# Four seven-product pairs instead of three in every second gate/up block, and plain pairs cut into halves, in a one-core float32 decoder layer

## The chip, the cores and the metric

The kernel runs on one core of a Trainium2 chip. Its time is device microseconds (us) from one launch; three runs gave 1085.74, 1085.87 and 1086.69 us, median 1085.87. Everything is computed to float32 accuracy: TensorE multiplies operands that were split into a high and a low part, and three matmuls make one product.

## The reference

A decoder layer for 256 tokens with width 2048: a combined input projection, a gated linear recurrence beside a retention head group, an output projection, and a SwiGLU feed-forward part of width 5632. The change concerns only the gate and up projections of the last part:

```
u = rmsnorm(h, ln2_w[l])
ff = jax.nn.silu(jnp.einsum('bsd,df->bsf', u, w_ffn_gate[l])) * jnp.einsum('bsd,df->bsf', u, w_ffn_up[l])
h = h + jnp.einsum('bsf,fd->bsd', ff, w_ffn_down[l])
```

with `u` 256x2048 and the gate and up weights 2048x5632 each, in float32.

## The kernel before

**Blocks, pairs and quads.** After the input part, the kernel is a list of blocks: two for the output projection (index 0 and 1), eleven for gate/up (index 2 to 12), two for the down projection. A gate/up block makes 512 gate and 512 up columns for all 256 tokens, in four PSUM banks c11, c12, c21 and c22 (token half by gate or up). It runs over the 2048 input rows in eight *pairs* of 128 rows each way; the weights of a pair are a *quad* of four 128x512 pieces, b11, b12, b22 and b21, loaded as two halves of 128x1024 (512 KB each).

**Products.** A *plain* pair takes eight products of a left piece (activations, 128x128) and a quad piece. A *summed* pair (table `SUMMED`) takes seven products, by sums of pieces on both sides. The sums of the left (s1 to s4) are made once and serve all blocks; the sums of the weights (t1 to t4) are made for each pair, by four VectorE additions in place (L648). A product is three matmuls in `three` (L670 high by high, L671 high by the low weights, L672 low by the high weights), so a plain pair has 24 matmuls and a summed one 21.

**Shared and direct steps.** The seven products of a summed pair stand in two places. Four of them are the *shared* step (`share`, 12 matmuls): they run one block ahead, while the block before is still accumulating in the other four banks, since they must be combined (L782 to L787) before plain products may be added to them. The other three are the *direct* step (`direct`, 9 matmuls), in the block itself; its pieces b22 and b21 are loaded a second time, and t4 is kept from the shared step. The string `STEPS` of a block gives the order: p a plain pair, s a shared step for the next block, d a direct step of this block.

**Making the weights ready.** Each piece is split by `split`: ScalarE casts the high part (L112), VectorE subtracts it from the raw weights for the low part (L113). Per pair this is:

- plain: two loads, two splits of 128x1024;
- shared: two loads, the split of b11 (128x512), the four additions, the splits of t1 with t3 (128x1024), of t2 and of t4 (128x512 each);
- direct: one load, one split of 128x1024.

The split pieces lie in pools of four buffers of 128x1024 for high (`wh`) and four for low parts (`wl`). A shared step holds two of each (b11 with t2, and t1 with t3), a direct step one, a plain pair two. t4 has buffers of its own. The raw weights have six buffers. A buffer is filled anew when the last instruction that reads it is done.

**What sets the order.** The program is written as a list of steps, with loads three halves ahead (`AHEAD`, L1086). A scheduler at build time then orders the instructions of each engine by its own estimate of times and gives out buffers as they come free; on the chip each engine runs its list in order and waits by semaphores. So three matmuls of one product may stand apart, and steps overlap by some matmuls.

Of the kernel before, what the change touches and what calls it, by code (L numbers as in the profile page):

```python
# [28 lines left out]

SUMMED = ((), (4, 5), (2, 3)) + ((1, 2, 3), (0, 1, 2, 3)) * 4 + ((1, 2, 3), (1, 2, 3))
SUMMED_OUT, SUMMED_FFN = (4, 5), (0, 1, 2, 3)

PLAIN = ((4, 5, 6, 7, 0, 1, 2, 3),) * 2 + (tuple(range(8)),) * 11
STEPS = ("pppspppspp", "ppspdpsdpp", "pdpsdpspspp") + ("pspsdpsdpsdp", "psdpsdpsddp") * 4 + ("psdpsdpsdpp", "psdpsdpsdpp")


EARLY_DOWN = (0, 1, 2)
# [5 lines left out]
def tile_hymba_layer(ctx: ExitStack, tc: tile.TileContext, A: dict, out: bass.AP):  # L45
# [17 lines left out]
    def nm(s):  # L63
        counter[0] += 1
        return f"{s}_{counter[0]}"
# [45 lines left out]
    def split(dst_h, dst_l, src):  # L111
        act.copy(out=dst_h, in_=src)  # L112
        v.tensor_tensor(out=dst_l, in0=src, in1=dst_h.bitcast(F32), op=ALU.subtract)  # L113

    class Unit:


        n_loads = 2

        def __init__(self, src, pieces=1, before=None, after=None):  # L120
            self.src, self.pieces, self.before, self.after = src, pieces, before, after
            self.h, self.l = [], []

        def load(self, j):
            raw = rpool.tile([P, 1024], F32, tag="raw", name=nm("raw"))
            h = wpool.tile([P, 1024], F32R, tag="wh", name=nm("wh"))
            l = wpool.tile([P, 1024], F32R, tag="wl", name=nm("wl"))
            n = 1024 // self.pieces
            for p in range(self.pieces):
                o = p * n  # L130
                nc.sync.dma_start(out=raw[:, o : o + n], in_=self.src[:, j * 1024 + o : j * 1024 + o + n])
                if self.before:
                    self.before(j * self.pieces + p)
            for p in range(self.pieces):
                o = p * n
                split(h[:, o : o + n], l[:, o : o + n], raw[:, o : o + n])
                if self.after:
                    self.after(j * self.pieces + p)
            self.h.append(h)
            self.l.append(l)  # L140
# [306 lines left out]
    half = {}  # L447
# [156 lines left out]
    class Quad:  # L604
# [3 lines left out]
        n_loads = 2  # L608
# [42 lines left out]
    EIGHT = (  # L651
        ("c11", "a11", "b11"), ("c12", "a11", "b12"), ("c22", "a21", "b12"), ("c21", "a21", "b11"),
        ("c11", "a12", "b21"), ("c12", "a12", "b22"), ("c22", "a22", "b22"), ("c21", "a22", "b21"),
    )
    LAST = tuple(e for c in ("c11", "c21", "c12", "c22") for e in EIGHT if e[0] == c)
# [7 lines left out]
    def room(m):  # L663

        return (aux, bank)[m % 2]
# [81 lines left out]
    class Direct(Quad):  # L747


        n_loads = 1  # L750
# [5 lines left out]
        def load(self, half):  # L756
# [2 lines left out]
            self.cut(("b22", "b21"), r)  # L759
            self.parts["t4"] = self.shared.parts["t4"]  # L760

    class Block:


# [25 lines left out]
            for c, a, b in DIRECT:  # L790
                three(self.ps[c], self.lefts[self.summed[m]][a], quad.parts[b], False, False, True)

        def plain(self, i, quad, first, last):
            ps, onto, seen = self.ps, bool(self.summed), set()
            for n, (c, a, b) in enumerate(LAST if last else EIGHT):
                if first and n == 4:
                    while turns:
                        turns.pop(0)()
                start = c not in ps
                if start:  # L800
                    ps[c] = room(self.index)(c)
                stop = last and c in seen
                three(ps[c], self.lefts[i][a], quad.parts[b], start, stop, onto)
                seen.add(c)
                if stop:
                    self.post(c, ps[c])

        def put(self, after):
            plain = [i for i in PLAIN[self.index] if i not in self.summed]
            for k, kind in enumerate(self.steps):  # L810
                if kind == "p":
                    i, n = plain.pop(0), len(plain)
                    quad = Quad(self.src(i), False)
                    run = lambda i=i, quad=quad, k=k, n=n: self.plain(i, quad, k == 0, n == 0)
                elif kind == "d":
                    m = self.steps[:k].count("d")
                    quad = Direct(self.shared[m])
                    run = lambda m=m, quad=quad: self.direct(m, quad)
                else:
                    m = self.steps[:k].count("s")  # L820
                    quad = after.shared[m]
                    run = lambda m=m: after.share(m)
                program.append(([quad], run))
# [209 lines left out]
    first = [True]  # L1033
# [31 lines left out]
    def swap():  # L1065
# [3 lines left out]

    blocks = [Block(d, lambda i, d=d: A["w_out"][8 * d + i], y, out_post(d), STEPS[d], SUMMED[d]) for d in range(2)]  # L1070
    blocks += [
        Block(2 + j, lambda i, j=j: A["w_gu"][8 * j + i], hh, ffn_post(j), STEPS[2 + j], SUMMED[2 + j])
        for j in range(NB)
# [15 lines left out]
    for step, (units, run) in enumerate(program):  # L1089
        need += sum(un.n_loads for un in units)  # L1090
        while done < min(len(loads), need + AHEAD):
            un, j = loads[done]
# [109 lines left out]
```

## Time and profile before

| | |
|---|---|
| median of three runs | 1085.87 us |
| span of the profiled execution (first to last instruction) | 1084.4 us |
| TensorE (PE) busy | 1074.2 us, 99%, 5101 matmuls |
| VectorE (DVE) busy | 953.5 us, 88%, 1371 instructions |
| ScalarE (ACT) busy | 660.9 us, 61%, 935 instructions |
| DMA read from HBM | 235.26 MB, 219 GB/s over the span |
| granted TensorE clock, mean | 0.999 |

The span is 1.5 us less than the median time; what lies before the first and behind the last instruction is not in it. Busy time of PE is time in which at least one matmul was running, and matmuls overlap: one takes about 0.39 us from start to end, but the next starts 0.23 us after it. The same holds in a small way for DVE: a 128x512 instruction lasts 0.69 us by the profile, and the next may start 0.60 us after it. Views by time stretch and the list of single instructions (start, duration, engine, line, operation, tiles) are used below; there the tile names stand without buffer numbers, so `wl<-raw,wh` is any split into a low part.

In the order of instructions, shown below and in the prediction's sense, names carry numbers: `c22_1343` is a bank, `wh_1330` and `wl_1331` are high and low split weights, `ah`/`al` the left operand's parts, `sh`/`sl` those of its sums, `t4h`/`t4l` the parts of t4, `raw_1357` loaded weights.

### The profile page before, as it was taken

What the parts mean: (1) busy time and instruction counts of PE and PEld (TensorE: products, weight loads), DVE (VectorE), ACT (ScalarE), POOL (GpSimd) and SP (SyncE); (2) the same over time, 40 slices, a digit from 0 to 9 for tenths busy, and PEclk for the clock granted to TensorE, in tenths of its full rate; (3) what the DMA queues carried; (4) which work ended last, traced back from release to release, by engine and by line L of the source; (5) the groups of instructions that cost most, each with busy time, mean ns of one, the idle gap of its engine ahead of it and who ended that gap; (6) DMA issues with size and microseconds to landing.
All of it is one profiled execution on the core that took longest, in us unless ns stands there. A gap on an engine that the chain in (4) does not pass through costs nothing.

```text
span 1084.4 us, 14584 instructions
## 1 busy us (share of the span) xinstructions
PE 1074.2 (99%) x5101; PEld 899.5 (83%) x5101; DVE 953.5 (88%) x1371; ACT 660.9 (61%) x935; POOL 51.0 (5%) x61
## 2 busy tenths in 40 slices
PE   9999999999999999999999999999999999999997
PEld 7888888888888788888888888888888888888885
DVE  7789799988878889888998998999899899898986
ACT  7666644468746676565566566556556666655563
POOL 0612230000000000000000000000000000000001
PEclk9999999999999999999999999999999999999999
DMA  9964474444565567577677677686675756465652
GB/s 330 333 211 168 160 252 173 174 175 171 181 230 205 184 228 275 198 248 266 220 245 261 220 264 235 233 289 214 233 271 194 265 181 213 171 214 199 212 209 85
DMA packets 69274, 238.32 MB, mean 220 GB/s; under 512 B 7888, under 2 KB 8272, under 8 KB 69200
## 3 DMA queue, kind: packets, MB, share of 16 engines
q1 hardware_dynamic: 68400, 235.29, 62.7%
q0 software_dynamic: 512, 1.57, 0.4%
q8 instruction: 40, 0.66, 0.2%
q10 hardware_dynamic: 288, 0.52, 0.1%
q14 instruction: 34, 0.28, 0.1%
HBM read 235.26 MB, written 2.10 MB: 219 GB/s over the span
## 4 chain that ended last, share of the span: by engine, by line
PE 97%; DVE 1%; issue 1%; DMA 0%; ACT 0%; POOL 0%; SPq 0%; POOLq 0%; ACTq 0%
PE c L670 22%; PE c L672 22%; PE c L671 22%; PE fm L184 11%; PE fm L186 5%; PE tm L164 3%; PE tm L165 3%; PE tm L166 3%; PE p L672 1%; PE p L671 1%; PE p L670 1%; PE ft L833 1%; DMA raw<-in_w_v 0%; PE ht L576 0%; PE sc L482 0%
## 5 line engine op out<-in xcount | busy, mean ns | idle before, releaser
L112 ACT CAST wh<-raw 128x1024 fp32r<-128x1024 f32 (+1 forms) x490 | 460.9, 965 | 362.6 <-PE c L672 132.5
L113 DVE TENSOR_TENSOR wl<-raw,wh 128x1024 fp32r<-128x1024 f32 (+1 forms) x490 | 538.2, 1122 | 91.2 <-ACT wh L112 88.4
L671 PE MATMUL c<-wl,ah 128*128 128x512 f32 x850 | 331.0, 390 | 0.0
L672 PE MATMUL c<-wh,al 128*128 128x512 f32 x850 | 330.4, 389 | 0.0
L670 PE MATMUL c<-wh,ah 128*128 128x512 f32 x850 | 275.0, 391 | 0.2 <-ACT wh L112 0.2
L670 PEld LDWEIGHTS c<-wh,ah 128*128 128x128 f32 x850 | 159.4, 188 | 33.4 <-ACT wh L112 1.1
L672 PEld LDWEIGHTS c<-wh,al 128*128 128x128 f32 x850 | 159.6, 188 | 33.0
L671 PEld LDWEIGHTS c<-wl,ah 128*128 128x128 f32 x850 | 159.6, 188 | 32.7
L184 PE MATMUL fm<-u,wh 128*128 128x512 f32 x512 | 161.3, 396 | 0.0
L186 PEld LDWEIGHTS fm<-u,wl 128*128 128x128 f32 x512 | 96.0, 188 | 22.5
L186 PE MATMUL fm<-u,wl 128*128 128x256 f32 x512 | 101.1, 278 | 0.0
L184 PEld LDWEIGHTS fm<-u,wh 128*128 128x128 f32 x512 | 78.4, 189 | 0.3
L648 DVE TENSOR_TENSOR raw<-raw,raw 128x512 f32<-128x512 f32 x106 | 73.1, 690 | 2.8
L648 DVE TENSOR_TENSOR raw<-raw 128x512 f32<-128x512 f32 x106 | 72.7, 689 | 2.4
L671 PE MATMUL c<-wl,sh 128*128 128x512 f32 x176 | 68.5, 389 | 0.0
L672 PE MATMUL c<-wh,sl 128*128 128x512 f32 x176 | 68.0, 389 | 0.0
L670 PE MATMUL c<-wh,sh 128*128 128x512 f32 x176 | 60.4, 394 | 0.3 <-ACT sh L112 0.3
L165 PE MATMUL tm<-wl,u 128*128 128x512 f32 x128 | 48.8, 394 | 0.0
L166 PE MATMUL tm<-wh,u 128*128 128x512 f32 x128 | 48.7, 390 | 0.0
L164 PE MATMUL tm<-wh,u 128*128 128x512 f32 x128 | 47.3, 398 | 0.8 <-ACT u L288 0.8
L954 POOL TENSOR_TENSOR htok<-htok,fw 128x512 f32<-128x512 f32 x2 | 2.5, 1273 | 895.9 <-ACT junk L947 895.9
L670 PEld LDWEIGHTS c<-wh,sh 128*128 128x128 f32 x176 | 33.1, 188 | 7.3 <-ACT sh L112 0.7
(245 smaller groups left out, 1034.9 us busy)
## 6 DMA issues: line engine op xcount, KB each, us to landing
raw<-in_w_gu SPq DMA_DIRECT2D x212, 512.0 KB, 5.5
raw<-in_w_down SPq DMA_DIRECT2D x91, 512.0 KB, 4.3
raw<-in_w_out SPq DMA_DIRECT2D x34, 512.0 KB, 3.7
raw<-in_w_lx SPq DMA_DIRECT2D x16, 512.0 KB, 6.3
raw<-in_w_k SPq DMA_DIRECT2D x16, 512.0 KB, 3.5
raw<-in_w_q SPq DMA_DIRECT2D x16, 512.0 KB, 4.0
raw<-in_w_rg SPq DMA_DIRECT2D x16, 512.0 KB, 3.4
raw<-in_w_lg SPq DMA_DIRECT2D x16, 512.0 KB, 3.4
```

The source lines that it names most:

```text
L112: act.copy(out=dst_h, in_=src)
L113: v.tensor_tensor(out=dst_l, in0=src, in1=dst_h.bitcast(F32), op=ALU.subtract)
L164: pe.matmul(ps, ah, wh, start=first, stop=False)
L165: pe.matmul(ps, ah, wl, start=False, stop=False)
L166: pe.matmul(ps, al, wh, start=False, stop=last)
L184: pe.matmul(ps, wh, hl, start=n + i == 0, stop=False)
L186: pe.matmul(ps[:, :S], wl, hl[:, :S], start=False, stop=n + i == len(order) - 1)
L648: v.tensor_tensor(out=dst, in0=a, in1=b, op=ALU.add)
L670: pe.matmul(p, ah, bh, start=first, stop=False, skip_group_check=onto)
L671: pe.matmul(p, ah, bl, start=False, stop=False, skip_group_check=onto)
L672: pe.matmul(p, al, bh, start=False, stop=last, skip_group_check=onto)
L833: pe.transpose(pt[:, o : o + P], g[:, (2 * b + c) * P : (2 * b + c) * P + P], ident)
```

## The change

`SUMMED` now gives four summed pairs (0 to 3) to each of the blocks 4 to 11; before, blocks 4, 6, 8 and 10 had four and blocks 3, 5, 7, 9 and 11 three (block 3 still has three, block 12 too). `STEPS` of the blocks 4 to 10 becomes one string, `psdhsdhsdhsdhp`: four shared, four direct, and four plain pairs, of which two go as halves. A new step kind h runs half of a plain pair, four of its eight products, on one of its two loaded halves (the first four products use b11 and b12, the last four b22 and b21).

```
-SUMMED = ((), (4, 5), (2, 3)) + ((1, 2, 3), (0, 1, 2, 3)) * 4 + ((1, 2, 3), (1, 2, 3))
+SUMMED = ((), (4, 5), (2, 3), (1, 2, 3)) + ((0, 1, 2, 3),) * 8 + ((1, 2, 3),)
...
-STEPS = ("pppspppspp", "ppspdpsdpp", "pdpsdpspspp") + ("pspsdpsdpsdp", "psdpsdpsddp") * 4 + ("psdpsdpsdpp", "psdpsdpsdpp")
+STEPS = ("pppspppspp", "ppspdpsdpp", "pdpsdpspspp", "pspsdpsdpsdp") + ("psdhsdhsdhsdhp",) * 7 + ("psdpsdpsddp", "psdpsdpsdpp")
...
+    class HalfOf:
+
+
+        n_loads = 1
+
+        def __init__(self, quad, half):
+            self.quad, self.half = quad, half
+
+        def load(self, j):
+            self.quad.load(self.half)
...
-        def plain(self, i, quad, first, last):
+        def plain(self, i, quad, first, last, some=slice(None)):
             ps, onto, seen = self.ps, bool(self.summed), set()
-            for n, (c, a, b) in enumerate(LAST if last else EIGHT):
+            for n, (c, a, b) in enumerate((LAST if last else EIGHT)[some]):
...
+                elif kind == "h":
+                    at = self.steps[:k].count("h") % 2
+                    if not at:
+                        i = plain.pop(0)
+                        whole = Quad(self.src(i), False)
+                    quad = HalfOf(whole, at)
+                    some = slice(4 * at, 4 * at + 4)
+                    run = lambda i=i, quad=whole, some=some: self.plain(i, quad, False, False, some)
```

Over the whole program PE has 12 matmuls fewer (4 pairs by 3), DVE 28 instructions more (for each of 4 pairs four additions and three splits), ACT 12 casts more, and the load queue (SP) 4 loads of 512 KB more (the second loading of b22 and b21).

The rows below show the two engines at the places that matter later. First DVE, one round of the middle of a block: before, of a round "s d p" (block 5).

```order
L113 TENSOR_TENSOR wl_1090_5275<-raw_1088_5272,wh_1089_5274 128x512
L648 TENSOR_TENSOR raw_1088_5272<-raw_1088_5272 128x512
L648 TENSOR_TENSOR raw_1088_5272<-raw_1088_5272,raw_1095_5294 128x512
L648 TENSOR_TENSOR raw_1095_5294<-raw_1088_5272,raw_1095_5294 128x512
L648 TENSOR_TENSOR raw_1095_5294<-raw_1095_5294 128x512
L113 TENSOR_TENSOR wl_1097_5303<-raw_1088_5272,wh_1096_5302 128x1024
L113 TENSOR_TENSOR wl_1102_5313<-raw_1100_5310,wh_1101_5312 128x1024
L113 TENSOR_TENSOR wl_1090_5275<-raw_1095_5294,wh_1089_5274 128x512
L113 TENSOR_TENSOR wl_1105_5343<-raw_1103_5340,wh_1104_5342 128x1024
L113 TENSOR_TENSOR t4l_1099_5307<-raw_1095_5294,t4h_1098_5306 128x512
L113 TENSOR_TENSOR wl_1108_5349<-raw_1106_5346,wh_1107_5348 128x1024
L113 TENSOR_TENSOR wl_1111_5367<-raw_1109_5364,wh_1110_5366 128x512
```

The round is b11, the four additions, t1 with t3, the direct piece, t2, a plain half, t4 and the second plain half; the last row is b11 of the next round. And now, of a round "s d h" (block 8):

```order
L113 TENSOR_TENSOR wl_1359_6499<-raw_1357_6496,wh_1358_6498 128x512
L648 TENSOR_TENSOR raw_1357_6496<-raw_1357_6496 128x512
L648 TENSOR_TENSOR raw_1357_6496<-raw_1357_6496,raw_1360_6514 128x512
L648 TENSOR_TENSOR raw_1360_6514<-raw_1357_6496,raw_1360_6514 128x512
L648 TENSOR_TENSOR raw_1360_6514<-raw_1360_6514 128x512
L113 TENSOR_TENSOR wl_1362_6523<-raw_1357_6496,wh_1361_6522 128x1024
L113 TENSOR_TENSOR wl_1367_6542<-raw_1365_6539,wh_1366_6541 128x1024
L113 TENSOR_TENSOR wl_1370_6560<-raw_1368_6557,wh_1369_6559 128x1024
L113 TENSOR_TENSOR wl_1359_6499<-raw_1360_6514,wh_1358_6498 128x512
L113 TENSOR_TENSOR t4l_1364_6527<-raw_1360_6514,t4h_1363_6526 128x512
L113 TENSOR_TENSOR wl_1373_6566<-raw_1371_6563,wh_1372_6565 128x512
```

One split of 128x1024 has gone from the round: only one half of a plain pair stands in it, and the next round's b11 follows at once.

Then PE, where the second shared step of a block is prepared. Before (block 5): the last matmuls that read a half of the plain pair that stands ahead (`wh_1079`), and 25 rows further on the first ones on the t1 and t3 of the second shared step.

```order
L672 MATMUL c22_1019_4943<-wh_1079_5224,al_834_4091 128x512
L671 MATMUL c21_1020_4947<-wl_1080_5225,ah_833_4090 128x512
L672 MATMUL c21_1020_4947<-wh_1079_5224,al_834_4091 128x512
L670 MATMUL c11_1018_4939<-wh_1086_5268,ah_833_4090 128x512
L670 MATMUL c12_1021_4951<-wh_1086_5268,ah_833_4090 128x512
```

```order
L670 MATMUL c22_1092_5282<-wh_1096_5302,sh_744_3682 128x512
L670 MATMUL c21_1093_5286<-wh_1096_5302,sh_744_3682 128x512
L670 MATMUL c11_1018_4939<-wh_1101_5312,ah_741_3673 128x512
L670 MATMUL c12_1021_4951<-wh_1101_5312,sh_744_3682 128x512
L670 MATMUL c12_1094_5290<-wh_1089_5274,sh_744_3682 128x512
L671 MATMUL c22_1092_5282<-wl_1097_5303,sh_744_3682 128x512
```

From the third row of the first piece to the last row of the second, the first read of the low parts of t1 and t3, it is 30 matmuls. The third row holds the last read of `wh_1079`; it is the first of the four `wh` buffers then in use to come free. The same two places now, in block 8 (`wh_1330` is the piece of the first direct step, the first buffer of the first round of which the last read comes):

```order
L671 MATMUL c11_1261_6058<-wl_1331_6378,ah_734_3652 128x512
L672 MATMUL c11_1261_6058<-wh_1330_6377,al_735_3653 128x512
L671 MATMUL c12_1264_6070<-wl_1331_6378,sh_737_3661 128x512
L672 MATMUL c12_1264_6070<-wh_1330_6377,sl_738_3662 128x512
L670 MATMUL c11_1261_6058<-wh_1337_6421,ah_837_4102 128x512
```

```order
L670 MATMUL c22_1343_6435<-wh_1347_6455,sh_744_3682 128x512
L670 MATMUL c21_1344_6439<-wh_1347_6455,sh_744_3682 128x512
L670 MATMUL c11_1261_6058<-wh_1352_6474,ah_741_3673 128x512
L670 MATMUL c12_1264_6070<-wh_1352_6474,sh_744_3682 128x512
L671 MATMUL c22_1343_6435<-wl_1348_6456,sh_744_3682 128x512
```

From the fourth row of the first piece to the last of the second it is now 27 matmuls. From there to the same row of the third round (`wl_1362`) it is 33 matmuls, the 12, 9 and 12 of a round "s d h", and 33 more to that of the fourth (`wl_1376`); before, a round "s d p" had 45. The blocks 4 to 10 have these rows alike.

## The prediction

> **What bounds the kernel now.** I read first how busy the engines are, then what PE waits for, then the stretches of two blocks in the middle.
>
> ```profile
> PE 1074.2 (99%) x5101; PEld 899.5 (83%) x5101; DVE 953.5 (88%) x1371; ACT 660.9 (61%) x935; POOL 51.0 (5%) x61
> PE warm L105 <- DVE eps_t L98: 1.1, 1, 1.1
> PE tm L164 <- ACT u L288: 0.8, 2, 0.5
> PE c L670 <- ACT sh L112: 0.3, 1, 0.3
> PE c L670 <- ACT wh L112: 0.2, 1, 0.2
> 510.50:558.10 47.60, 47.60 (x215) 39.45 (x215) 43.73 (x55) 28.45 (x37) 0.00 (x0) 1.00 0.73 243
> 558.10:594.60 36.50, 36.50 (x166) 30.26 (x166) 32.37 (x42) 21.43 (x29) 0.00 (x0) 1.00 0.72 247
> ```
>
> The second to fifth rows are all that PE waits for: 2.4 us in the whole span, nothing of it in the gate/up blocks beyond single tenths. In the last two rows (length; busy PE, weight loads, DVE, ACT, POOL; clock, DMA share, GB/s) PE is busy throughout, in a block that computes shared steps for four pairs (47.6 us) and in one that computes them for three (36.5 us). DVE is free for 3.87 and 4.13 us of them. So a matmul less is time less, as long as DVE and ACT deliver the split weights before PE asks for them. Whether they still do is the question.
>
> **What the change removes from PE.** Twelve matmuls. Their pace comes from two starts 45 matmuls apart, the first reads of t1 and t3 in two successive rounds "s d p":
>
> ```profile
> 533.21 0.39 PE L671 MATMUL c<-wl,sh 128*128 128x512 f32 x1
> 543.41 0.39 PE L671 MATMUL c<-wl,sh 128*128 128x512 f32 x1
> ```
>
> 10.20 us / 45 = 0.2267 us. 12 x 0.2267 = **2.7 us less**, if nothing stalls. The two stretches together are 84.1 us with 363 matmuls of products and 16 transposes. Two blocks of the changed kind have 360, so 83.4 us, 41.7 us a block.
>
> **What it adds to DVE.** One round on DVE, as it stands in the trace of block 5:
>
> ```profile
> 527.49 0.69 DVE L113 TENSOR_TENSOR wl<-raw,wh 128x512 fp32r<-128x512 f32 x1 [1.83 <-ACT wh L112]
> 528.21 0.69 DVE L648 TENSOR_TENSOR raw<-raw 128x512 f32<-128x512 f32 x1
> 528.94 1.42 DVE L648 TENSOR_TENSOR raw<-raw,raw 128x512 f32<-128x512 f32 x2
> 530.39 0.69 DVE L648 TENSOR_TENSOR raw<-raw 128x512 f32<-128x512 f32 x1
> 531.00 1.22 DVE L113 TENSOR_TENSOR wl<-raw,wh 128x1024 fp32r<-128x1024 f32 x1
> ...
> 535.01 0.68 DVE L113 TENSOR_TENSOR t4l<-raw,t4h 128x512 fp32r<-128x512 f32 x1
> 535.61 1.22 DVE L113 TENSOR_TENSOR wl<-raw,wh 128x1024 fp32r<-128x1024 f32 x1
> ```
>
> b11 and the four additions take 3.51 us (527.49 to 531.00). Then come, back to back, three splits of 128x1024 and one of 128x512 up to 535.01, and t4 to 535.61: t4 takes 0.60, so with t2 at 0.60 too the three take (4.01 - 0.60) / 3 = 1.14 each. From 527.49 to 535.61 it is **8.12 us**, and the same ten instructions, in a slightly other order, are the whole round "s d h" of the changed kernel. PE has 12 + 9 + 12 = 33 matmuls in that round, **7.48 us**. So DVE loses 0.64 us to PE in every round. In the round "s d p" DVE has one split more, 9.26 us, against 45 matmuls in 10.20 us, and gains 0.94.
>
> Over a block this is covered. A summed pair costs DVE 3.51 + 2 x 0.60 = 4.7 us more than a plain one (the splits of 128x1024 are two in either), four of them are added over eight blocks, 2.35 us a block on the mean 38.05 of the two stretches: 40.4 us of 41.7. The plain pairs at the two ends of the string (10.9 us of PE, 4.6 us of splits) have to give back what the rounds between them lose. ACT's 12 further casts and the 4 loads (2 MB, 0.9% of the bytes) change no such sum: ACT is at 28.45 of 47.6 us where it is busiest in these rows.
>
> **Why the plain pairs cannot give it back ahead.** DVE could enter the rounds far ahead of PE, but the split weights have four buffers. In a round, two belong to the shared step, one to the direct piece, one to the half. So b11 of the second round cannot be split until PE frees a buffer of the first. The trace of block 5 has this very step:
>
> ```profile
> 526.41 0.39 PE L672 MATMUL c<-wh,al 128*128 128x512 f32 x1
> 526.83 0.62 ACT L112 CAST wh<-raw 128x512 fp32r<-128x512 f32 x1 [2.14 <-PE c L672]
> ```
>
> The last matmul on the old buffer starts at 526.41, the cast at 526.83 after 2.14 us of waiting, DVE at 527.49 after waiting too (row above). DVE is 1.08 us behind the freeing matmul, t1 and t3 are split at 531.00 + 1.22 = 532.22, and PE reads them at 533.21, 30 matmuls after 526.41: 0.99 us to spare. In the changed order the first buffer to come free has its last read 27 matmuls ahead of that same read. Three matmuls less are 0.68 us: **0.31 us to spare** at the second round. It doesn't help to be earlier: following DVE through the end of the block (the splits of the last and first plain pair, and the additions of the next first shared step, each held by the buffers that PE frees one by one) I have it done with the first round's work over 1 us ahead of that cast, and idle, as it is for 1.83 us here.
>
> From there it is a race without refill. Second round: 0.31 to spare. Third: 0.31 - 0.64 = 0.33 late. Fourth: 0.97 late, about 1.0 with the handing over. What is late is the split of t1 and t3, and behind it on DVE, in order, the direct piece and the half, which PE wants later by 1.6 us and more; ACT's casts for them wait behind the cast of the same sums and come out even with it. After the fourth round the last plain pair's splits have two rounds' worth of cover, DVE recovers, and waits again for the buffer that starts the next block's second round. So each block pays once: **1.0 us x 7 blocks = 7.0 us**. Bounds: not below 0 (with a spare of 1.28 us at the second round nothing is ever late), and not above 2.1 us a block (if b11 got the buffer whose last read comes five matmuls later, 1.13 us). I take 1.0 since both ends of that step were measured in one and the same mechanism, and only three matmuls were counted off.
>
> Sum: 1084.4 - 2.7 + 7.0 = 1088.7 us of span. The median of the runs is 1.5 us above the span, so **1090.2 us**, slower by 0.4%.
>
> [...]
>
> **Rivals.**
>
> *DVE keeps up (not slower).* The mechanism is the entry into the second round: if the buffer of b11 there comes free 1 us earlier than I count, DVE's idle time before it turns into lead, 1.28 us are to spare, and the whole 2.7 us are won: 1083.2 us. For it: 1.3 us a block are left over, and before, the same entry never cost PE anything. Against: four buffers, and none of the four is read for the last time earlier. It decides from a spare of 1.28 us upward.
>
> *DVE is late, but little.* If the spare is 0.99 us as in block 5, the third round is just in time and the fourth 0.3 us late: 7 x 0.3 = 2.1 us, against 2.7: 1085.3 us. For it: that is the measured spare; against: the three matmuls.
>
> *The loads are late as well.* A raw buffer goes back when its splits are done, and the load behind it must land before ACT's cast.
>
> ```profile
> SPq L628 <- DVE wl L113: 325.9, 168, 7.5
> raw<-in_w_gu SPq DMA_DIRECT2D x212, 512.0 KB, 5.5
> ```
>
> SP waits for DVE's splits, so a late DVE issues late. The half's load can be issued when the direct piece is split, 3.51 + 2 x 1.14 = 5.8 us into a round, and is cast about 4.2 us into the next, 12.3 us: 6.5 us for a median landing of 5.5. If half of the rounds ran over by some 0.7 us, three rounds would add 1 us to each block, 7 us in all: 1097 us. Against: a round asks for 2.1 MB in 8.12 us, 258 GB/s, and the stretches above run at 243 to 247 on the mean, and PE never waits in them.
>
> *Instructions do not overlap on DVE when it has no slack.* Durations instead of starts, 7 x 0.69 + 3 x 1.22 = 8.5 us a round: 1.0 us lost per round, 2 x 1.0 - 0.3 = 1.7 a block, 12 in all: 1095.3 us. Against: the rows above were back to back already. [...]
>
> **How the numbers follow.** The forecast has a chance of 0.60, DVE in time 0.16, late but little 0.15, late loads 0.07, no overlap 0.02. A measurement of this kernel can tell about 0.2%, 2.2 us, from no change. Of the forecast's own range, 1087.5 to 1092.5, a small part (0.05) lies within 2.2 us of before. So faster 0.17 (the first rival and a little), same 0.19, slower 0.64. The range reaches from the first rival to stalls of 1.5 us a block, 1085.9 - 2.7 + 10.5: **1083.0 to 1093.7 us**.
>
> **What would show it.** PE should have 12 matmuls fewer, and waits of about 1 us in each of the blocks 4 to 10, none elsewhere: `c L671` waiting for DVE `wl L113` or `c L670` for ACT `wh L112`, at the third and fourth round of the block, with gaps near 0.3 and 0.6 us. DVE should be without a break from the second round's b11 to the last plain pair, and idle for over 1 us ahead of that b11. The stretch of one block should be near 42.7 us. No gap on PE would say that the entry is earlier than I count; gaps also at the second round, that it is later; ACT waiting for DMA, that loads are the cause.

## The result, and the profile after

The changed kernel takes **1093.0 us** (median of 4 runs, 1092.8 to 1093.5), the kernel before 1085.9 us (4 runs, 1085.7 to 1086.7). The ratio is **1.0065**, with a 95% interval of 1.0052 to 1.0078: slower by 7.1 us. The span of the profiled execution went from 1084.4 to 1091.1 us, by 6.7 us.

First the page of the changed kernel, the span and the busy times:

```profile
span 1091.1 us, 14619 instructions
PE 1076.1 (99%) x5089; PEld 894.0 (82%) x5089; DVE 969.8 (89%) x1399; ACT 667.2 (61%) x947; POOL 50.8 (5%) x61
```

PE has the 12 matmuls less (5101 before), and yet 1.9 us more of busy time and a longer span. What PE waits for (total us, times, longest):

```profile
PE c L670 <- ACT wh L112: 3.9, 16, 0.9
PE tm L164 <- ACT u L288: 1.7, 2, 1.2
PE warm L105 <- DVE eps_t L98: 1.1, 1, 1.1
PE c L670 <- ACT sh L112: 0.3, 1, 0.3
```

The first row is new in this size: before, it was 0.2 us and one time. It has 16 waits, two in each of the seven blocks 4 to 10, and two more. These totals are smaller than what the waits cost, because a matmul counts as running for 0.39 us while the next one could start 0.23 us after it. The cost shows in the distance of starts, below.

The stretches of blocks 7 and 8 (length; busy PE, weight loads, DVE, ACT, POOL; clock, DMA share, GB/s):

```profile
602.40:645.30 42.90, 42.50 (x190) 34.18 (x189) 40.19 (x51) 25.83 (x35) 0.00 (x0) 1.00 0.73 246
645.30:688.20 42.90, 42.50 (x190) 34.19 (x189) 40.21 (x52) 25.57 (x35) 0.00 (x0) 1.00 0.73 245
```

A block now takes 42.9 us, 1.15 us more than the 41.7 that its 180 product matmuls and 8 transposes need at the pace of before. (Of the 1.15, 0.1 is no stall: the same number of matmuls takes 41.8 us a block in the last experiment, where PE doesn't wait.) DVE is busy for 40.2 us of it and free for 2.7.

Where this happens is seen in the list of single instructions of block 8 (start, duration, engine, line, operation, tiles; in brackets the idle time ahead and who ended it). DVE, from the entry into the second round on:

```profile
656.90 1.22 DVE L113 TENSOR_TENSOR wl<-raw,wh 128x1024 fp32r<-128x1024 f32 x1
659.84 0.69 DVE L113 TENSOR_TENSOR wl<-raw,wh 128x512 fp32r<-128x512 f32 x1 [1.72 <-ACT wh L112]
663.35 1.22 DVE L113 TENSOR_TENSOR wl<-raw,wh 128x1024 fp32r<-128x1024 f32 x1
667.36 0.69 DVE L113 TENSOR_TENSOR t4l<-raw,t4h 128x512 fp32r<-128x512 f32 x1
667.96 0.69 DVE L113 TENSOR_TENSOR wl<-raw,wh 128x512 fp32r<-128x512 f32 x1
```

ACT, the cast behind that entry, and the casts in the third round (x4 are four casts in a row: t1 with t3, the direct piece, the half, t2):

```profile
659.18 0.62 ACT L112 CAST wh<-raw 128x512 fp32r<-128x512 f32 x1 [1.76 <-PE c L672]
670.21 3.47 ACT L112 CAST wh<-raw 128x1024 fp32r<-128x1024 f32 x4 [3.60 <-DVE raw L648]
```

PE, its first read of the second round's t1 and t3, and its stalls in the third and fourth round:

```profile
664.87 0.39 PE L671 MATMUL c<-wl,sh 128*128 128x512 f32 x1
...
671.45 0.63 PE L670 MATMUL c<-wh,sh 128*128 128x512 f32 x2
672.26 0.50 PE L670 MATMUL c<-wh,ah 128*128 128x512 f32 x1 [0.18 <-ACT wh L112]
672.60 0.40 PE L670 MATMUL c<-wh,sh 128*128 128x512 f32 x1
...
680.38 0.50 PE L670 MATMUL c<-wh,ah 128*128 128x512 f32 x1 [0.21 <-ACT wh L112]
680.71 0.40 PE L670 MATMUL c<-wh,sh 128*128 128x512 f32 x1
```

Read together: DVE has done the first round's work at 658.12 (656.90 + 1.22) and sits idle for 1.72 us, because ACT's cast of b11 waits for the buffer that PE reads. The split of t1 and t3 ends at 663.35 + 1.22 = 664.57, PE reads it at 664.87: **0.30 us to spare**. From one b11 to the next DVE takes 667.96 - 659.84 = **8.12 us** without a break. In the third round PE's second matmul of the row with x2 starts at 671.68, the next at 672.26 instead of 671.90 (0.35 us late), and the one behind it 0.34 us after that instead of 0.23 (0.11 us more). The fourth round loses 0.10 + 0.38 + 0.11 in the same way. Together 1.05 us per block. What PE waits for there is ACT's cast of the direct piece; that cast stands behind the cast of the sums, which waits for DVE's additions (3.60 us `<-DVE raw L648`).

There is one more stall, of 1.07 + 0.11 us, in block 12, which makes the first shared step of the down projection. Here is PE, a matmul's start at 822.26 and the next at 823.56:

```profile
822.26 0.39 PE L672 MATMUL c<-t4h,al 128*128 128x512 f32 x1
823.56 0.50 PE L670 MATMUL c<-wh,ah 128*128 128x512 f32 x1 [0.91 <-ACT wh L112]
```

and ACT ahead of it:

```profile
819.16 0.62 ACT L112 CAST sh<-s 128x512 fp32r<-128x512 f32 x1 [3.53 <-DVE s L554]
821.95 2.51 ACT L112 CAST wh<-raw 128x512 fp32r<-128x512 f32 x3
```

The down projection works on other left operands than the gate/up blocks (its own `ah`, `al` and the sums `sh`, `sl`). They are made at this very place, and ACT sits idle for 3.53 us until DVE has the sums, with the casts of weights queued behind. Before, block 11 had three summed pairs and one plain pair more behind each other, and no stall there.

The bill of the span: -2.7 (matmuls) + 7 x 1.15 (blocks 4 to 10) + 1.2 (block 12) = +6.5, of 6.7 measured.

### The profile page after: what moved, and what is told of

Same layout as the page of the kernel before. It is cut to its first block, busy times and chain, and to the rows that moved or that the text cites. A ratio compares the mean times of both kernels' runs of the same rounds, so it can differ in the third digit from the quotient of the medians.

```text
span 1091.1 us, 14619 instructions
## 1 busy us (share of the span) xinstructions
PE 1076.1 (99%) x5089; PEld 894.0 (82%) x5089; DVE 969.8 (89%) x1399; ACT 667.2 (61%) x947; POOL 50.8 (5%) x61
## 3 DMA queue, kind: packets, MB, share of 16 engines
q0 software_dynamic: 512, 1.57, 0.4%
## 4 chain that ended last, share of the span: by engine, by line
PE 93%; ACT 2%; DVE 2%; DMA 1%; issue 1%; POOL 0%; SPq 0%; ACTq 0%; POOLq 0%
PE c L670 21%; PE c L672 21%; PE c L671 21%; PE fm L184 11%; PE fm L186 5%; PE tm L164 3%; PE tm L166 3%; PE tm L165 3%; ACT wh L112 2%; PE p L672 1%; PE p L671 1%; PE p L670 1%; PE ft L852 1%; DVE wl L113 1%; DVE raw L648 1%
## 5 line engine op out<-in xcount | busy, mean ns | idle before, releaser
L112 ACT CAST wh<-raw 128x1024 fp32r<-128x1024 f32 (+1 forms) x498 | 465.8, 959 | 358.0 <-DVE raw L648 130.6
L671 PE MATMUL c<-wl,ah 128*128 128x512 f32 x826 | 322.1, 390 | 0.0
L672 PE MATMUL c<-wh,al 128*128 128x512 f32 x826 | 321.7, 390 | 0.0
L670 PE MATMUL c<-wh,ah 128*128 128x512 f32 x826 | 275.8, 393 | 3.9 <-ACT wh L112 3.9
L670 PEld LDWEIGHTS c<-wh,ah 128*128 128x128 f32 x826 | 155.0, 188 | 42.1 <-ACT wh L112 11.3
L671 PEld LDWEIGHTS c<-wl,ah 128*128 128x128 f32 x826 | 155.2, 188 | 31.7
L648 DVE TENSOR_TENSOR raw<-raw,raw 128x512 f32<-128x512 f32 x114 | 78.8, 691 | 2.9
L648 DVE TENSOR_TENSOR raw<-raw 128x512 f32<-128x512 f32 x114 | 78.4, 690 | 2.7
L671 PE MATMUL c<-wl,sh 128*128 128x512 f32 x192 | 75.1, 391 | 0.0
L672 PE MATMUL c<-wh,sl 128*128 128x512 f32 x192 | 74.4, 390 | 0.0
L670 PE MATMUL c<-wh,sh 128*128 128x512 f32 x192 | 69.8, 399 | 0.3 <-ACT sh L112 0.3
L671 PEld LDWEIGHTS c<-wl,sh 128*128 128x128 f32 x192 | 36.1, 188 | 9.5 <-DVE wl L113 2.6
```

What stands on the lines that cost most here:

```text
L648: v.tensor_tensor(out=dst, in0=a, in1=b, op=ALU.add)
L670: pe.matmul(p, ah, bh, start=first, stop=False, skip_group_check=onto)
L671: pe.matmul(p, ah, bl, start=False, stop=False, skip_group_check=onto)
L672: pe.matmul(p, al, bh, start=False, stop=last, skip_group_check=onto)
```

## The experiments

The theory is that of the prediction: a round "s d h" costs DVE 0.64 us more than PE; the four split buffers let DVE enter the second round with only 0.31 us to spare; so PE stalls in the third and fourth round. The first rival says that DVE has too much work on the whole, whatever the order; the second, that loads are late. All ratios are against the kernel before, run in the same series (medians there 1086.2 to 1086.7 us), with their 95% intervals.

The table gives for each experiment the *spare* at a shared step, that is, the time from the end of DVE's split of t1 and t3 to PE's first read of it (0.30 above). It is worked out from two rows of the lists of single instructions each time, as above. The steps are those that a block's string names, in its order. Where PE has stalled just ahead of that read, the same difference comes out at 0.13 to 0.15, so 0.15 in the table means just in time at best:

| kernel | 1st s | 2nd s | 3rd s | 4th s | block, us |
|---|---|---|---|---|---|
| the change | 2.53 | 0.31 | stalls | stalls | 42.86 |
| halves in the second round | 1.57 | 0.31 | 1.48 | 0.61 | 42.36 |
| halves in the first round | 1.57 | 1.69 | 0.75 | 0.15 | 42.4 |
| short t4 addition | 2.23 | 0.70 | 0.32 | 0.32, stalls | 42.27 |
| cover by the string | 0.9 to 1.7 | 0.99 | 0.15 | 0.45 to 0.49 | 41.8 |

### A fifth split buffer, in the changed kernel and in the one before

```
+            from_pool = extra[0][1] if self.extra else wpool
-            h, l = (wpool.tile([P, 1024], F32R, tag=g, name=nm(g)) for g in ("wh", "wl"))
+            h, l = (from_pool.tile([P, 1024], F32R, tag=g, name=nm(g)) for g in ("wh", "wl"))
...
+                    quad.extra = 4 <= self.index <= 11
```

The direct steps of blocks 4 to 11 take their split buffer from a pool of one buffer of its own; the four are left to the rest.

In the changed kernel:

> The changed kernel, with a fifth buffer of split weights, high and low, for the direct steps of blocks 4 to 11, in the space that the final norm's weights take later; nothing is left out. Theory (the race of a round on four buffers): b11 of the second round no longer waits for the first direct piece, DVE's 1.3 us to spare per block become lead, and the waits of PE of 1.1 us a block go, 7 x 1.15 = 8 us; the 1.2 us at block 12 stay: 1085 us. Rival A (DVE has too much work over a whole block, whatever the buffers): 1093 as the changed kernel. Rival B (loads land late): 1093.

And the same in the kernel before:

> The kernel before with the same fifth buffer. PE waited for nothing there, so by every theory nothing changes: 1085.9 us, within 0.1%.

Measured: 1102.6 us, ratio 1.0146 (1.0132 to 1.0159), for the changed kernel; 1101.6 us, 1.0137 (1.0123 to 1.0151), for the one before. Both missed by far, and the second shows why: the buffer alone made the kernel before 15 us slower. PE's waits in it, and its clock:

```profile
PE c L671 <- ACT c L786: 4.5, 3, 1.7
PE c L672 <- DVE wl L113: 1.5, 2, 0.8
PE c L671 <- ACT wh L112: 1.4, 2, 1.2
core 0: 1097.9 us, clock 0.993
```

PE's products now begin with L671 instead of L670: the build-time scheduler, given another buffer, put all engines' instructions in another order, and in it PE waits for the combination of the shared banks (`c L786` is its copy of c12 in that kernel). The waits are not all of the 15 us: the granted clock of this kernel's four runs was 0.991 to 0.994, that of the kernel before in the same series 0.997 to 0.999; if matmuls slow down in proportion, that half of a per cent is an estimated 5 us. So the runs do not answer the question they were made for. That the change costs only 1.0 us on this base (1102.6 - 1101.6) agrees with the theory, but on a base with other stalls and another clock (0.993, against 0.997 in the changed kernel with the buffer) it proves nothing.

### b11 out of the four buffers, in both kernels

```
-                h, l = self.hl = [wpool.tile([P, 1024], F32R, tag=g, name=nm(g)) for g in ("wh", "wl")]
-                self.parts["b11"] = h[:, :512], l[:, :512]
+                self.parts["b11"] = act_tile("bh", F32R), act_tile("bl", F32R)
...
             self.add(r)
+            h, l = self.hl = [wpool.tile([P, 1024], F32R, tag=g, name=nm(g)) for g in ("wh", "wl")]
```

> The changed kernel, but b11 of each shared step is split into buffers of the activations' pool, not into the four of the split weights; t2 takes one of the four when the additions are done. Nothing is left out, and DVE and ACT have the same instructions. Theory (entry on four buffers): b11 and the additions of the second round no longer wait for the first direct piece, which is 4.6 us of the 5.8 from the freeing matmul to the sums, so DVE's idle time before that entry goes and PE's waits at the third and fourth round with it: 8 us less, 1085 (the 1.2 us at block 12 stay). Rival A (DVE's total work over a block): 1093. Rival B (loads): 1093.

> The kernel before with b11 apart in the same way: PE waited for nothing, so nothing changes by any theory: 1086 us within 0.1%.

Measured: 1098.3 us, 1.0111 (1.0097 to 1.0125), and 1092.6 us, 1.0062 (1.0048 to 1.0076). Again the base moved. PE's main waits in it, three and up to 2.1 us long, are new in this size:

```profile
PE c L670 <- ACT wh L112: 3.4, 3, 2.1
```

But these waits (at 373, 405 and 844 us) stand outside the blocks 4 to 10, and inside them the run does show something. What ACT's casts of weights wait for buffers that PE still reads, from 474 to 774 us, first in the changed kernel, then with b11 apart:

```profile
ACT wh L112 <- PE c L672: 30.3, 26, 1.8
...
ACT wh L112 <- PE c L672: 0.6, 2, 0.3
```

and DVE at the entry into a second round with b11 apart, without the 1.72 us of idle time:

```profile
617.02 1.22 DVE L113 TENSOR_TENSOR wl<-raw,wh 128x1024 fp32r<-128x1024 f32 x1
618.17 0.69 DVE L113 TENSOR_TENSOR bl<-raw,bh 128x512 fp32r<-128x512 f32 x1
```

So it is the four buffers that hold DVE at this entry. The stall in the third round is gone, and one of 0.8 us in the fourth is left: t2 is now split ahead of t1 and t3, DVE waits 0.26 us in each round for ACT, and a round takes it 8.65 us (first additions at 627.55 and 636.20) instead of 8.12. The seven blocks together take 298.8 us instead of 300.1; the kernel as a whole is slower than the change by what it loses outside them. What a fifth buffer alone would bring stays open: no run here changed the number of buffers and left the order as it was.

### The halves alone, without more summed pairs

`SUMMED` as before (four and three pairs in turn, no matmul saved), the halves in blocks 4 to 9:

```
-STEPS = ... ("pspsdpsdpsdp", "psdpsdpsddp") * 4 + ...
+STEPS = ... "pspsdpsdpsdp") + ("psdhsdhsdhdhp", "pshsdhsdhsdhpp") * 3 + ("psdpsdpsddp", ...
```

> The pairs of the kernel before (three and four in turn), but in blocks 4 to 9 two plain pairs of each go as halves between shared and direct steps: psdhsdhsdhdhp and pshsdhsdhsdhpp. No matmul, no DVE instruction and no load more or less than before. Theory: the rounds s d h are there, 7.48 us of PE against 8.12 of DVE, so PE waits in the third (and, where there are four shared steps, in the fourth) round: 0.4 us a block with three, 1.0 with four, 3 x 0.4 + 3 x 1.0 = 4 us: 1090. Rival A (DVE's total work): 1085.9, since the totals are those of before. Rival B (loads): 1085.9 to 1087.

Measured: 1087.1 us, 1.0010 (1.0000 to 1.0019). PE's waits:

```profile
PE tm L164 <- ACT u L288: 0.8, 2, 0.6
PE c L670 <- ACT wh L112: 0.4, 2, 0.2
PE c L670 <- ACT sh L112: 0.3, 1, 0.3
```

So the rounds "s d h" alone do not make the loss; I had expected 1090. The spares show why: 3.40, 1.29, 1.03, 0.39 in a block that makes four shared steps, 1.21 at the entry in the other. The two rounds behind one another still lose 0.64 us (1.03 - 0.39), as in the prediction, but this order enters the race with 1.2 to 1.3 us, and so nothing runs out. Only block 4 waits, 0.36 + 0.11 us, and it is the test within the run: it has the same string as the blocks 6 and 8, but stands behind another one and enters with 0.30 us (493.10 to 493.40), where block 6 has 1.22. My expectation had taken the entry of 0.31 over from the changed kernel. The loss takes both: the drift, and a late entry.

### t4's addition on POOL

```
-                v.tensor_tensor(out=dst, in0=a, in1=b, op=ALU.add)
+                (pool if dst is b21 else v).tensor_tensor(out=dst, in0=a, in1=b, op=ALU.add)
```

> The changed kernel, but the fourth addition of each shared step (t4, not needed before the next block) on POOL instead of DVE; nothing is left out. Theory: the round on DVE shrinks by 0.61 to 7.51 us, as long as PE's 7.48, so with 0.3 us to spare at the second round nothing is late any more: 1085 us, if POOL's addition doesn't slow DVE. Rival A: the block's total falls by 2.4 us, also 1085. Rival B: the raw buffer is given back later, 1093 or more.

Measured: 1109.8 us, 1.0216 (1.0202 to 1.0230). DVE had one addition less to do per round, and yet was slower. The groups of this kernel in blocks 4 to 10 (count; busy us, mean ns; idle before):

```profile
L648 POOL TENSOR_TENSOR raw<-raw 128x512 f32<-128x512 f32 x28 | 36.2, 1293 | 275.3 <-DVE raw L648 250.6 <-DMA raw<-in_w_gu 24.7
L113 DVE TENSOR_TENSOR wl<-raw,wh 128x1024 fp32r<-128x1024 f32 x114 | 157.2, 1417 | 16.5 <-ACT wh L112 16.5
```

and the same DVE splits in the changed kernel:

```profile
L113 DVE TENSOR_TENSOR wl<-raw,wh 128x1024 fp32r<-128x1024 f32 x113 | 133.7, 1220 | 3.8 <-ACT wh L112 3.8
```

While POOL adds, DVE's split of t1 and t3 takes longer. One round of this kernel on POOL:

```profile
644.61 1.29 POOL L648 TENSOR_TENSOR raw<-raw 128x512 f32<-128x512 f32 x1 [7.47 <-DVE raw L648]
```

and on DVE, first one round, then all splits of blocks 4 to 10 (ns, shortest/median/longest):

```profile
644.95 4.91 DVE L113 TENSOR_TENSOR wl<-raw,wh 128x1024 fp32r<-128x1024 f32 x4 [0.47 <-ACT wh L112]
...
L113 DVE TENSOR_TENSOR wl<-raw,wh x170: 674/1210/2065, 473.2 to 787.6; 128x1024 fp32r<-128x1024 f32 x114, 128x512 fp32r<-128x512 f32 x56
```

Four splits take 4.91 us instead of 4.09, 0.82 us more, and the longest one 2065 ns instead of 1220. The split starts at 644.95 and POOL is done at 645.90; 645.90 + 1.22 is 647.12, and the split ended at about 644.95 + 2.07 = 647.02. So it ended as if it had made nearly no headway until POOL was done: of the 0.95 us in which both ran, 0.82 were lost. In the groups above, the 114 splits of 128x1024 took a mean of 1417 ns instead of 1220, which is 0.80 us for each of the 28 additions. That is more than the 0.61 us that the addition had cost on DVE (662.74 to 663.35 in the change). What held the split back is not shown by any run here. There is a second loss in the same row: DVE waits 0.47 us for ACT's cast of t1 and t3, a time that the fourth addition had filled. A round took DVE 8.76 us (first additions at 633.58 and 642.34). So the run cannot tell the theory from its rivals; DVE became slower instead of freer.

### The fourth addition left out, and the fourth addition shortened

First left out:

```
-            for dst, a, b in ((b11, b11, b12), (b12, b12, b22), (b22, b11, b22), (b21, b22, b21)):
+            for dst, a, b in ((b11, b11, b12), (b12, b12, b22), (b22, b11, b22)):
```

> The changed kernel without the fourth addition (t4) of every shared step: this leaves out a part of the computation, so t4 is b21 alone. DVE has 0.61 us less in a round, 7.51 us against PE's 7.48. Theory (race of the round after a late entry): with 0.3 us to spare at the entry nothing is late in the third and fourth round: 1085 us. Rival A (total): 2.4 us less a block, also 1085. Rival B (loads): 1093. Beside the run in which POOL made this addition it also tells what POOL's part cost DVE.

Measured: 1090.7 us, 1.0038 (1.0026 to 1.0051), less slow than the change by 2.3 us and not by the 8 expected. The addition's time was not DVE's to win. ACT starts its cast of t1 and t3 behind the second addition, and DVE's third and fourth additions run beside it; without the fourth, DVE stands idle until the cast is done:

```profile
670.98 3.50 DVE L113 TENSOR_TENSOR wl<-raw,wh 128x1024 fp32r<-128x1024 f32 x3 [0.47 <-ACT wh L112]
```

A round still takes DVE 7.95 us or more (first additions at 625.58 and 633.53) and not 7.51, so it loses at least 0.47 us to PE and the stalls stay. Besides, t4's piece now depended on its load alone, so the scheduler put its cast far ahead, and there ACT waited for the load, 9.0 us in all. ACT's waits:

```profile
ACT t4h L112 <- DMA raw<-in_w_gu: 9.0, 12, 1.7
```

About half of the 2.3 us is won in the blocks 4 to 10 (298.9 us instead of 300.1), the rest around block 12, where the stall is absent.

The next run kept the dependence and made the addition short instead:

```
+                n = 64 if dst is b21 and len(self.parts) < 2 else 512
-                v.tensor_tensor(out=dst, in0=a, in1=b, op=ALU.add)
+                v.tensor_tensor(out=dst[:, :n], in0=a[:, :n], in1=b[:, :n], op=ALU.add)
```

> The changed kernel with the fourth addition (t4) of each shared step made on 64 of its 512 columns: this leaves out 7/8 of that addition, but the split of t4 still waits for it, unlike the run without it. DVE has about 0.47 us less in a round, 7.65 against PE's 7.48. Theory: the loss per round falls from 0.64 to 0.17, so the wait in the third round goes and that in the fourth shrinks to 0.1: 1093.0 - 6.5 = 1086.5. Rival A (total): 1.9 us less a block, so also about 1086. Rival B (loads): 1093.

Measured: 1088.4 us, 1.0017 (1.0008 to 1.0026), with a block of 42.27 us. The stall in the third round is gone (0.08 us are left of 0.46), the one in the fourth is 0.33 + 0.11. A quicker round on DVE, with not a buffer and not a matmul changed, takes away half of the loss in each block. That agrees with a race between the two, but the first rival expected the same, so this run doesn't separate them. The gain is 4.6 us, not the 6.5 that I expected, and part of it is the stall in block 12, which is absent here too. The entry rose to 0.70, and a round took DVE 7.95 us (b11 at 623.77 and 631.72), not 7.65, since it now waits for ACT's cast of t1 and t3 here as well:

```profile
534.60 4.10 DVE L113 TENSOR_TENSOR wl<-raw,wh 128x1024 fp32r<-128x1024 f32 x4 [0.21 <-ACT wh L112]
```

### Seven blocks instead of eight

Block 11 has three summed pairs as before, so that what stands ahead of block 12 is as before:

```
-... ((0, 1, 2, 3),) * 8 + ((1, 2, 3),)
+... ((0, 1, 2, 3),) * 7 + ((1, 2, 3),) * 2
-... ("psdhsdhsdhsdhp",) * 7 + ("psdpsdpsddp", "psdpsdpsdpp")
+... ("psdhsdhsdhsdhp",) * 6 + ("psdpsdpsddp", "psdpsdpsdpp", "psdpsdpsdpp")
```

> The changed kernel with block 11 as before: three summed pairs and psdpsdpsdpp, block 10 with psdpsdpsddp; blocks 4 to 9 keep the new string. 3 matmuls more than the changed kernel (0.7 us). Theory: one block less with the 1.15 us of waits, and the wait of 1.2 us at the start of block 12, where the left operands of the down part are made beside the sums, goes: 1093.0 + 0.7 - 1.15 - 1.2 = 1091.4. If the wait at block 12 has to do with the number of blocks only, it stays: 1092.6.

Measured: 1091.2 us, 1.0045 (1.0032 to 1.0058), as expected. The wait of 0.9 us in block 12 is gone, and the longest of this row is now 0.2:

```profile
PE c L670 <- ACT wh L112: 2.6, 13, 0.2
```

The sum: 9 matmuls fewer than before are -2.0, six blocks at 1.15 are +6.9, together +4.9; measured against the median of before in that series, 1091.22 - 1086.27 = +4.95.

### The same work in another order: both halves in one round

Four summed pairs in eight blocks, as in the change, the same instructions on DVE; only the string differs. Both halves behind the second direct step:

```
-("psdhsdhsdhsdhp",) * 7
+("psdhsdhhsdhsdp",) * 7
```

> The changed kernel with one half moved: psdhsdhhsdhsdp in blocks 4 to 10, so that the second round has both halves of a pair (45 matmuls of PE, 10.2 us, against 9.26 us of DVE) and the fourth has none but is followed by the last plain pair. No instruction more or less, the same four buffers, the same work of DVE per block. Theory (late entry and then a race of rounds): DVE gains 0.94 in the second round, loses 0.64 in the third, so it has 0.6 us to spare where PE now waits: the 1.15 us of waits a block go, 1093.0 - 8.0 = 1085.0, at most 1087 if a third of them stays. Rival A (DVE's total work over a block): 1093. Rival B (loads): 1093.

And behind the first:

```
-("psdhsdhsdhsdhp",) * 7
+("psdhhsdhsdhsdp",) * 7
```

> The changed kernel with the same half moved to the first round instead: psdhhsdhsdhsdp. Theory: the first round stands ahead of the entry that waits for a buffer, so cover there is given to an idle DVE; the second and third rounds are s d h still and lose 0.64 each, so PE goes on waiting in the third and fourth round, 0.3 to 1.0 us a block by the spare at the entry: 1088 to 1092. Rival A: 1093. Rival B: 1093.

Measured: 1089.1 us, 1.0026 (1.0015 to 1.0036), and 1089.8 us, 1.0033 (1.0020 to 1.0045). In both, the stalls of the change are gone: none of the spares runs out (table above). In the first, the round with two halves refills 0.31 to 1.48, and the next takes 0.87 away. In the second the entry has 1.69, and two rounds take 0.94 and 0.60. So 40 us of DVE work in a block do fit, and the first rival falls. (In the fourth round of the second run it is only just so: with a spare of 0.15, some 0.02 us are lost there.) What keeps both kernels slower than before is another wait, which I had not foreseen. PE of the first of the two, its waits:

```profile
PE c L670 <- ACT c L796: 2.0, 7, 0.3
PE c L670 <- ACT wh L112: 1.1, 2, 0.9
```

and the place in block 7:

```profile
600.91 0.39 PE L672 MATMUL c<-wh,sl 128*128 128x512 f32 x1
...
604.08 0.39 PE L672 MATMUL c<-wh,al 128*128 128x512 f32 x1
604.76 0.50 PE L670 MATMUL c<-wh,ah 128*128 128x512 f32 x1 [0.29 <-ACT c L796]
```

What PE waits for, on DVE:

```profile
602.20 0.68 DVE L794 TENSOR_TENSOR p<-c,p 128x512 f32<-128x512 f32 x1
...
603.40 0.68 DVE L795 TENSOR_TENSOR q<-p,c 128x512 f32<-128x512 f32 x1
```

and on ACT:

```profile
604.12 0.59 ACT L796 COPY c<-q 128x512 f32<-128x512 f32 x1 [0.83 <-DVE q L795]
```

From the last matmul of the last shared step (600.91) to the first plain product on the combined bank, the combination takes 604.76 - 600.91 = 3.85 us, over two engines; a part of it is that DVE has splits of weights in its list ahead of the first and between the two subtractions (at 601.06 and 602.80). The string ends in "sdp", and only 15 matmuls stand between; 15 x 0.2267 = 3.40. That leaves 0.45 us, and 0.11 with the slower start behind it, in every block. The change, with "sdhp", has 12 matmuls more there, 27, and no such wait. The bill, by the length of a block as for the change, is -2.7 + 7 x (42.36 - 41.7) + 1.2 (block 12) = +3.1 for the first of the two and, at 42.4, +3.4 for the second; measured were 1089.14 - 1086.68 = +2.5 and +3.1. The second's time fell within what I expected, but for another reason than the one I had given.

### A string that covers both waits

From these runs a string can be put together: both halves in the first round (the entry with spare), two direct steps at the end (cover for the combination), block 11 as before (no stall at block 12). It saves 9 matmuls instead of 12:

```
-... ((0, 1, 2, 3),) * 8 + ((1, 2, 3),)
+... ((0, 1, 2, 3),) * 7 + ((1, 2, 3),) * 2
-... ("psdhsdhsdhsdhp",) * 7 + ("psdpsdpsddp", "psdpsdpsdpp")
+... ("pshhsdhsdhsddp",) * 6 + ("psdpsdpsddp", "psdpsdpsdpp", "psdpsdpsdpp")
```

> Four summed pairs in the seven blocks 4 to 10 and three in block 11 as in the run with seven blocks, 9 matmuls less than before (2.0 us), and in blocks 4 to 9 the string pshhsdhsdhsddp: both halves of a pair behind the first shared step, where the run with the halves in the first round had 1.7 us to spare at the second round, and two direct steps behind the last shared step, so that 33 matmuls stand between it and the first plain product on its combined banks (27 in the changed kernel, 15 in the two runs with moved halves, which wait there). Nothing is left out. Theory (a race of rounds from a given spare, and the cover of the combination): no wait in blocks 4 to 10 and at block 12, so 1086.3 - 2.0 = 1084.3, within 0.8. Rival A (DVE's total work over a block, 40.4 us of 41.7): waits of about 1 us stay in each of the six blocks, 1090.

Measured: **1084.8 us** (11 runs, 1084.3 to 1085.8), before in that series 1086.5 us (15 runs, 1085.4 to 1086.9); ratio 0.9989 (0.9980 to 0.9998). The page and the waits:

```profile
span 1082.9 us, 14617 instructions
...
PE tm L164 <- ACT u L288: 0.6, 2, 0.4
PE c L670 <- ACT sh L112: 0.3, 1, 0.3
PE c L670 <- ACT wh L112: 0.2, 1, 0.2
```

No wait is left that the kernel before didn't have, and the blocks 4 to 9 do the same work per block as in the change, on DVE too. The entry with 0.99 us was enough here, though the prediction's count needs 1.28 for two rounds of 33 matmuls: in the order that the scheduler gave, 32 matmuls stand between the first reads of the second and third round and 37 between those of the third and fourth (619.54, 626.81 and 635.24). The gain of 1.7 us is about what 9 matmuls are worth (2.0), and it is at the edge of what can be told from no change; the interval lies just below 1. It is the one of these kernels that beats both, and not by much.

## Why the prediction was right, and where it was not

It said slower, 1090.2 us, and the mechanism held point by point; the time came out 2.8 us higher.

- *PE saves 2.7 us.* Held: 12 matmuls fewer, and where nothing stalls the pace is the same.
- *A round takes DVE 8.12 us, against 7.48 on PE.* Held to the hundredth (659.84 to 667.96). The rival in which DVE's instructions don't overlap would have given 8.5, by durations of 0.69 and 1.22 us. The starts in this round stand closer: 0.60 us from t4's split to the next, and 1.14 between splits of 128x1024 (663.35 to 667.36 is 4.01, less 0.60 for t2, over three).
- *0.31 us to spare at the entry into the second round, and DVE idle ahead of it.* Held: 0.30, after 1.72 us of idleness ("over 1 us"). That buffers set this entry is read from the trace (ACT's cast of b11 waits 1.76 us for PE, DVE for ACT) and from the size, which came out; and with b11 out of the four buffers DVE's idle time there is gone. That one buffer more would cure the stall is not shown. That the late entry matters is shown: the same rounds entered with 1.2 us or more (halves alone, halves in the first round) do not stall, and block 4 of the halves alone, entered with 0.30, does.
- *0.33 us late in the third round, 0.97 in the fourth, 1.0 per block.* The sizes: 0.46 and 0.59, with 0.1 besides 1.15 per block. Each stall costs some 0.1 us more than the lateness, as the matmul behind the waiting one starts 0.34 us after it instead of 0.23. The term "1.0 us x 7 blocks = 7.0 us" was 8.0, and 7.35 of it are stalls.
- *Who is waited for.* I had named DVE's split of t1 and t3, or ACT's casts, which "come out even with it". It is ACT's cast of the direct piece alone. It stands behind the cast of the sums and is held by the same additions of DVE, so the cause is the same.
- *Waits in blocks 4 to 10, "none elsewhere".* This step failed. The sum had no term for the end of the gate/up part. I had followed DVE through a block whose left operands were ready. Block 11's string was changed too, from "psdpsdpsdpp" to "psdpsdpsddp", and block 12 behind it is where the left operands of the down projection are made. It cost 1.2 us; the seven-block run takes it away. The string alone doesn't make this stall: the run with the short t4 addition has the same strings and no such stall. What else must meet there stays open.
- *The remainder.* 0.2 us of the span, and 0.3 since the time of a run lies 1.8 us above the span here (1092.92 for the profiled execution) and not 1.5. 1.0 + 1.2 + 0.2 + 0.3 = 2.7 of the 2.8 us.

Of the rivals, "DVE keeps up" decided from a spare of 1.28 us upward, and the runs that had about that much (1.2 to 1.7) bear this out; the change didn't have it. The point itself holds only where 33 matmuls stand between the rounds, as the last string shows with 0.99. "The loads are late as well" doesn't show: in the stalls ACT waits for DVE's additions, not for DMA. That DVE has simply too much to do falls with the runs that do the same work in another order, above all the last, which has no wait in these blocks. One thing the prediction left out shows in the runs that shorten the fourth addition: in the change ACT's cast of t1 and t3 (from 662.07, 1.05 us) is done only some 0.2 us before DVE turns to them at 663.35, so a quicker DVE wins little before ACT sets the pace.

## What to carry to other kernels

Compare two engines over the shortest stretch in which a stall can't be made good, here one round, and not over the block: DVE had 2.7 us free in each block and still made PE wait 1.05. Ask then how far ahead the faster one can get before the race, which is what buffers decide, and count for every wait in the new order, the seldom ones too (a combination of banks, a change of operands), how many matmuls stand in front of it. And where a scheduler at build time sets the order, "one buffer more" is not a change of one thing: it moved the kernel before by 15 us in the wrong direction, with new waits and a lower clock (0.991 to 0.994, against 0.997 to 0.999).

## What was not expected of the hardware

- A DVE split of 128x1024 that ran beside an addition on POOL of 128x512 (1293 ns) took up to 2065 ns instead of 1220. In the round that was looked at, 0.82 of the 0.95 us in which both ran were lost, and 0.80 us for each of the 28 additions in the mean.
- A matmul that had to wait is followed at 0.33 to 0.34 us instead of 0.23, so a stall on PE costs 0.10 to 0.11 us beyond the wait itself, in every stall that was looked at (third round, fourth round and block 12 of the change, the combination with the halves moved).
